# Attention's last products and the first part of its output projection on one Trainium2 core

## The chip, the cores and the metric

The kernel runs on one core of one Trainium2 chip. The metric is the device time of one execution in microseconds (us). Work is spread over TensorE (PE, with its weight loads as PEld), VectorE (DVE), ScalarE (ACT), GpSimd (POOL) and the queue of SyncE (SP), which issues every DMA of this kernel. Each engine runs its instructions in the order in which they were put on it, and waits on semaphores for the others.

## The reference

A trunk of two encoder layers over 1024 tokens of width 1024, all in float32. Only the end of the first layer's attention and the start of the cross-attention behind it matter here:

```python
o = lax.map(attend_block, qb)            # softmax(q k^T) v, 16 heads, 4 key/value heads
o = o.transpose(1, 0, 4, 2, 3, 5).reshape(b, s, N_HEADS * HEAD_DIM)
return o @ w_o                           # output projection, 1024 x 1024
...
x = x + axial_gqa_attention(rmsnorm(x, attn_norm[ia]), ...)
x = x + memory_cross_attention(rmsnorm(x, xattn_norm[i]), ...)
```

`rmsnorm` scales each row by one over its root mean square and each channel by a factor; the factors of the norm ahead of the cross-attention are `xattn_norm`.

## The kernel before

Products of two float32 matrices are made of three passes: each operand is split into a high part (ACT copies it to the reduced type, line 673 or 665) and a low part (DVE subtracts the high part from the source, line 674 or 668), and `mm3` adds high x high, high x low and low x high (lines 746 to 748). Weights come by DMA into a buffer `scr` of 128 x 1024, of which there are six (line 657), and are split from there into slots `R`.

**The attention loop** (lines 1168 to 1211) runs over 128 units: a block of 128 queries, a head. `skewed` puts the stages of several units side by side. In step s stand: the scores of unit s (PE, four matmuls into one of two banks `pA`, line 779), with the row maximum (DVE, line 789), the exponential (ACT, line 792), the reciprocal of the sum (DVE, line 794) and the scaling of the probabilities by it (POOL, line 795); the transposes of unit s-2 (PE, eight, line 740) with their split into `PT` (lines 673 and 674); and, for every second unit, the values of units s-3 and s-4 (PE, 16 matmuls into a bank `pB`, of which there are four, lines 1192 and 1193), copied out by ACT (line 1198). Two heads are then joined: a DMA on SP's queue moves 64 partitions ("crossed", line 1200), POOL adds (line 1202) and splits the pair into the left operand of the projection, `OT` (lines 1205 and 1206). So POOL has the scaling and the joining in one queue. The loop is not ordered by hand: a list scheduler of the framework takes the instructions in program order and places them by its own model, so the order on each engine around a change can differ from the text's.

**Behind the loop** `run` (lines 2118 to 2141) loads and splits the first half of the projection's weights (`load_rows`, four pieces of 512 KB, line 681), then the rows `X` of the residual (eight tiles, line 2128) with the second half's four pieces after the first two tiles, and calls `cross`, which loads the factors `xattn_norm` by a broadcast DMA (`bcast`, line 712) before its planned section.

**The projection** is interleaved with the first work of the cross-attention (`Seven.begin`, line 447). For each step (n, t) - half n of the columns, row tile t - there are `gemm` (24 matmuls into a `pB` bank), `add` (DVE adds the bank to X[t], line 1556), `save` (a store of that half of X[t] to HBM, line 314), and after n = 1 the sum of squares of the row (ACT, line 727; POOL, lines 719 and 721), the normalisation in place (DVE, line 318) and the transposes (PE, line 323). The steps start with (0, 0), (0, 2), (1, 0), (1, 2); X[0]'s transposes follow the fourth. The normalisation overwrites X[0], so it waits for both stores of X[0].

Of the kernel before, what the change touches and what calls it, by code (L numbers as in the profile page):

```python
# [10 lines left out]
F32 = mybir.dt.float32  # L11
# [5 lines left out]
P = 128  # L17
D = 1024
S = 1024
NT = S // P  # L20
# [4 lines left out]
NH = 16  # L25
# [603 lines left out]
class Kernel:  # L629
# [64 lines left out]
    def R_(self, s):  # L694
        return self.R.tiles[s] if isinstance(s, int) else s

    def load_rows(self, w, n):

        slots = [self.R.get() for _ in range(4)]
        src = w[:, n * 512:(n + 1) * 512].rearrange("(k p) n -> p k n", p=P)  # L700
        for g in range(2):
            h, l = (self.R.v(s, 4) for s in slots[2 * g:2 * g + 2])
            for k in range(2):
                self.load_w(h[:, 2 * k:2 * k + 2], l[:, 2 * k:2 * k + 2],
                            src[:, 4 * g + 2 * k:4 * g + 2 * k + 2, :], 2)
        return slots

    def bcast(self, row):

# [49 lines left out]
        return self.R.v(h, 4)[:, k % 4, cols], self.R.v(l, 4)[:, k % 4, cols]  # L759


    def attention(self):
# [6 lines left out]
        Q, prs, OT, sums = {}, {}, [], {}  # L769

        def score(u):
            j, hh, i = units[u]
# [397 lines left out]
        with tc.tile_pool(name="at", bufs=1, reuse_waits="tile") as at:  # L1170
            PT = [[at.tile([P, 2048], F32R, name=f"PT{i}{j}") for j in range(2)] for i in range(2)]
            halves = self.scr().rearrange("p (a b c) -> p a b c", a=2, b=2)
            def parts(u):
                return (x.rearrange("p (a b) -> p a b", a=8) for x in PT[u // 2 % 2])

            def turn_p(u):
                ph, pl = parts(u)
                c = slice(u % 2 * P, (u % 2 + 1) * P)
                self.transposed(prs.pop(u), lambda g, p: self.hi_lo(ph[:, 4 * g:4 * g + 4, c], pl[:, 4 * g:4 * g + 4, c], p))

            def values(u):
                j, hh, i = units[u]
                if i == 0:
                    return
                kv = hh // 4
                if hh == 0:
                    OT.append([R.get(), R.get()])
                ph, pl = parts(u)
                o = self.psB()[:, :256]
                for kt in range(NT):  # L1190
                    v = R.tiles[V[kt // 4]].rearrange("p (k h c) -> p k h c", k=4, h=4)[:, kt % 4, kv, :]
                    nc.tensor.matmul(o, v, ph[:, kt], start=kt == 0, stop=False)  # L1192
                    nc.tensor.matmul(o, v, pl[:, kt], start=False, stop=kt == NT - 1)  # L1193
# [6 lines left out]
                nc.sync.dma_start(out=far[mine], in_=own[other])  # L1200
# [12 lines left out]
        return OT  # L1213


    def memory_part(self, mT, g, t):
# [6 lines left out]
    def cross(self, i, X, steps=None, mixer=None, over={}):  # L1223

        nc, R, a = self.nc, self.R, self.a
        Xd = self.tc.dram_tile([S, D], F32, name=f"Xq{i}")
        U = Seven(self, a["xattn_w_q"][i], lambda f: (2 * f * P, (2 * f + 1) * P), X, Xd, self.bcast(a["xattn_norm"][i]))
# [9 lines left out]
        def plan_split(plan, name, f, late):  # L1239
# [877 lines left out]

    def run(self):
        nc, R, a = self.nc, self.R, self.a
        OT = self.attention()  # L2120
        ws = [self.load_rows(a["attn_w_o"][0], 0)]
        xp = self.ctx.enter_context(self.tc.tile_pool(name="xres", bufs=1, reuse_waits="tile"))
        X = [xp.tile([P, D], F32, name=f"X{t}") for t in range(NT)]
        for t in (0, 2, None, 4, 6, 1, 3, 5, 7):
            if t is None:
                ws.append(self.load_rows(a["attn_w_o"][0], 1))
            else:
                nc.sync.dma_start(out=X[t], in_=a["x"][0][t * P:(t + 1) * P, :])
# [8 lines left out]
        steps = self.rows_by(lhs, X, free, lambda n, k: self.blk(ws[n], k, slice(0, 512)), lambda n: R.put(*ws[n]))  # L2137
        lhs, *ops = self.cross(0, X, steps)
        ready = []
        gemm, add, over = self.ffn(0, lhs, X, *ops, lambda plan: ready.extend([self.pool_weights(plan)]))  # L2140
        lhs, *ops = self.cross(1, X, None, partial(self.pool_mixer, gemm, add, ready[0]), over)
        self.ffn(1, lhs, X, *ops, out=self.out[0])


# [30 lines left out]
```

## Time and profile before

| | us |
|---|---|
| three runs, median (lowest to highest) | 2510.43 (2509.54 to 2513.05) |
| the profiled execution | 2508.51 |
| its span | 2506.7 |
| PE busy | 2473.4 (99%) |
| DVE busy | 1958.6 (78%) |
| ACT busy | 1348.4 (54%) |
| attention loop, about | 160 to 528 |
| projection's first four products | 528.8 to 551.0 |

Times in the profile are us from the start of the span. A row of the timeline gives start, length, engine, line, operation, output and inputs, count, and in brackets how long the engine stood idle before it and what released it. "SPq" rows are issues of DMAs; where several are merged, the length runs from the first to the last. In a table by stage each stretch has the busy time of PE, PEld, DVE, ACT and POOL, the mean granted clock of TensorE (1.00 is full speed), the share of the 16 DMA engines and GB/s. Of a wait for several semaphores only the last to come is named.

### The profile page before, as it was taken

To read this page: it belongs to the slowest core of one execution; us is meant where nothing else is said; L and a number is where in the kernel's file an instruction comes from. 1 tells how busy PE (TensorE), PEld (TensorE's weight loads), DVE (VectorE), ACT (ScalarE), POOL (GpSimd) and SP (SyncE) were. 2 spreads that over 40 slices of the span, in tenths; PEclk is the share of its full clock that TensorE was granted. 3 is DMA by queue.
4 is the path that set the end of the run, shared out by engine and by line. 5 is a ranking of instruction groups with operands and counts; after the bars stand their busy time and mean duration, and the time that the engine had idled before them with its cause. 6 is when DMAs were issued, how large, how long until landed. Compare 5 with 4: busy or idle time off the path is not lost.

```text
span 2506.7 us, 37225 instructions
## 1 busy us (share of the span) xinstructions
PE 2473.4 (99%) x13435; PEld 2129.7 (85%) x13435; DVE 1958.6 (78%) x2899; ACT 1348.4 (54%) x2307; POOL 436.2 (17%) x594
## 2 busy tenths in 40 slices
PE   9999999999999999999999999999999999999998
PEld 8999999978898888888888888889888888887887
DVE  7779989864986379888889776987559888888875
ACT  6558888852655255555555334655335555554542
POOL 5756666631011000000000003102010000000001
PEclk9999999999999999999999999999999999999999
DMA  7100000042595124243258553388223324337852
GB/s 253 43 2 14 13 14 13 13 171 68 187 317 183 57 79 126 84 122 110 85 170 285 198 182 111 126 283 306 73 72 109 114 84 124 108 93 255 278 189 97
DMA packets 314733, 326.50 MB, mean 130 GB/s; under 512 B 14133, under 2 KB 248861, under 8 KB 314549
## 3 DMA queue, kind: packets, MB, share of 16 engines
q1 hardware_dynamic: 314549, 324.12, 39.9%
q8 instruction: 106, 1.74, 0.3%
q14 instruction: 78, 0.64, 0.1%
HBM read 232.48 MB, written 82.58 MB: 126 GB/s over the span
## 4 chain that ended last, share of the span: by engine, by line
PE 87%; issue 4%; DVE 3%; DMA 2%; ACT 2%; POOL 1%; SPq 0%; POOLq 0%; DVEq 0%; ACTq 0%
PE pB L746 21%; PE pB L748 21%; PE pB L747 21%; PE pA L779 4%; PE pB L740 4%; PE pA L748 3%; PE pA L746 3%; PE pA L747 3%; PE pB L1193 2%; PE pB L1192 2%; DVE R L668 1%; PE pB L323 1%; ACT R L665 1%; DMA scr<-in_ffn_w_down 1%; PE pA L2058 1%
## 5 line engine op out<-in xcount | busy, mean ns | idle before, releaser
L746 PE MATMUL pB<-R,R 128*128 128x512 f32 (+1 forms) x2764 | 1024.3, 371 | 8.4 <-DVE scr L439 3.3
L748 PE MATMUL pB<-R,R 128*128 128x512 f32 (+1 forms) x2760 | 1016.4, 368 | 1.3 <-DVE R L668 1.2
L747 PE MATMUL pB<-R,R 128*128 128x512 f32 (+1 forms) x2764 | 1017.3, 368 | 0.0
L746 PEld LDWEIGHTS pB<-R,R 128*128 128x128 f32 x2764 | 521.1, 189 | 100.7 <-DVE scr L439 4.6
L748 PEld LDWEIGHTS pB<-R,R 128*128 128x128 f32 x2760 | 520.1, 188 | 89.0 <-DVE R L668 2.6
L747 PEld LDWEIGHTS pB<-R,R 128*128 128x128 f32 x2764 | 521.2, 189 | 85.6 <-DVE R L674 0.4
L665 ACT ACTIVATE R<-scr 128x512 fp32r<-128x512 f32 (+2 forms) x340 | 256.9, 781 | 218.3 <-DMA scr<-Gs 60.3
L668 DVE TENSOR_TENSOR R<-scr,R 128x512 fp32r<-128x512 f32 (+2 forms) x340 | 291.6, 887 | 21.5 <-ACT R L665 20.9
L668 DVE TENSOR_TENSOR R<-X,R 128x512 fp32r<-128x512 f32 x374 | 252.5, 686 | 67.5 <-ACT R L665 66.6
L665 ACT ACTIVATE R<-X 128x512 fp32r<-128x512 f32 x374 | 231.7, 630 | 135.8 <-PE pB L747 65.4
L719 POOL TENSOR_SCALAR ms<-ss 128x1 f32<-128x1 f32 (+1 forms) x53 | 14.9, 281 | 1659.0 <-ACT R L727 1280.7
L437 ACT COPY scr<-pB 128x512 f32<-128x512 f32 x156 | 91.3, 585 | 188.3 <-PE pB L748 182.5
L673 ACT ACTIVATE PT<-pB 128x512 fp32r<-128x512 f32 x256 | 140.1, 604 | 56.0 <-PE pB L740 55.7
L789 DVE TENSOR_REDUCE nm<-pA 128x1 f32<-128x1024 f32 x125 | 152.5, 1220 | 20.5 <-PE pA L779 20.5
L674 DVE TENSOR_TENSOR PT<-pB,PT 128x512 fp32r<-128x512 f32 x256 | 163.5, 679 | 5.0 <-ACT PT L673 4.9
L1765 DVE TENSOR_TENSOR X<-pB,X 128x512 f32<-128x512 f32 (+1 forms) x145 | 99.3, 686 | 85.5 <-PE pB L748 84.5
L795 POOL TENSOR_SCALAR scr<-scr,inv 128x1024 f32<-128x1024 f32 x125 | 140.7, 1127 | 70.1 <-DVE inv L794 69.8
L746 PE MATMUL pA<-R,R 128*128 128x512 f32 (+1 forms) x420 | 150.6, 359 | 0.0
L748 PE MATMUL pA<-R,R 128*128 128x512 f32 (+1 forms) x420 | 150.2, 358 | 0.2 <-DVE R L668 0.2
L747 PE MATMUL pA<-R,R 128*128 128x512 f32 (+1 forms) x420 | 150.0, 357 | 0.0
L779 PE MATMUL pA<-R,R 128*128 128x512 f32 x512 | 145.4, 405 | 0.0
L792 ACT ACTIVATE scr<-pA,nm 128x1024 f32<-128x1024 f32 x125 | 139.8, 1118 | 1.5 <-DVE nm L789 0.5
(172 smaller groups left out, 3485.0 us busy)
## 6 DMA issues: line engine op xcount, KB each, us to landing
X<-in_ffn_w_up SPq DMA_DIRECT2D x82, 512.0 KB
Gs<-X SPq DMA_DIRECT2D x105, 256.0 KB
scr<-in_ffn_w_down SPq DMA_DIRECT2D x45, 512.0 KB
scr<-Gs SPq DMA_DIRECT2D x35, 512.0 KB
scr<-in_xattn_w_kv SPq DMA_DIRECT2D x32, 512.0 KB
scr<-Gs SPq DMA_DIRECT2D x42, 384.0 KB
Wt<-scr SPq DMA_DIRECT2D x44, 256.0 KB
Gs<-scr SPq DMA_DIRECT2D x42, 256.0 KB
```

The source lines that it names most:

```text
L665: self.nc.scalar.activation(hi, src, AF.Copy)
L668: self.nc.vector.tensor_tensor(out=lo, in0=src, in1=hi.bitcast(F32), op=OP.subtract)
L673: nc.scalar.activation(hi, src, AF.Copy)
L674: nc.vector.tensor_tensor(out=lo, in0=src, in1=hi.bitcast(F32), op=OP.subtract)
L740: self.nc.tensor.transpose(p[:, k, :], src[:, b * P:(b + 1) * P], self.ident)
L746: mm(out, ah, bh, start=start, stop=False)
L747: mm(out, ah, bl, start=False, stop=False)
L748: mm(out, al, bh, start=False, stop=stop)
L779: nc.tensor.matmul(s[:, kh * 512:(kh + 1) * 512], q, R.v(K[part][kh], 4)[:, kv], start=part == 0, stop=part == 1)
L789: nc.vector.tensor_reduce(nm, s, axis=AX.X, op=OP.max, negate=True)
L792: nc.scalar.activation(pr, s, AF.Exp, bias=nm, accum_out=rs)
L795: nc.gpsimd.tensor_scalar(pr, pr, ri, 1.0, op0=OP.mult, op1=OP.mult)
```

## The change

Two products of the projection, steps (0, 0) and (0, 2), move into the attention loop's last steps (its drain): a fifth stage of `skewed` calls what `ahead` holds for a unit, one step after its values. The first half's weight pieces hang there too, at units 112, 115, 118 and 121, with load and split together; the two products hang at units 124 and 125. `load_rows` returns four calls, one for each piece, instead of doing all at once. `steps` then skips the products already made, and their adds and saves stay where they were. The first cross-attention's factors are loaded in `run` right behind the second half's weights, among the row loads in the text; the second layer's call of `bcast` moves to the caller, to the same place in the program.

```diff
-    def load_rows(self, w, n):
-        slots = [self.R.get() for _ in range(4)]
+    def load_rows(self, w, n, slots):
         src = w[:, n * 512:(n + 1) * 512].rearrange("(k p) n -> p k n", p=P)
...
+        def part(k):
+            if not slots:
+                slots.extend(self.R.get() for _ in range(4))
+            h, l = (self.R.v(s, 4)[:, 2 * k % 4:2 * k % 4 + 2] for s in slots[k // 2 * 2:k // 2 * 2 + 2])
+            self.load_w(h, l, src[:, 2 * k:2 * k + 2, :], 2)
+        return [partial(part, k) for k in range(4)]
...
-            skewed(len(units), (0, scores), (2, turn_p), (3, values))
+            skewed(len(units), (0, scores), (2, turn_p), (3, values), (4, lambda u: ahead.get(u, lambda: None)()))
...
-        OT = self.attention()
-        ws = [self.load_rows(a["attn_w_o"][0], 0)]
+        OT, X, wo, ws, early = [], [], a["attn_w_o"][0], [[], []], ((0, 0), (0, 2))
...
+        gemm, *others = self.rows_by(lhs, X, free, lambda n, k: self.blk(ws[n], k, slice(0, 512)), lambda n: R.put(*ws[n]))
+        first, second = (self.load_rows(wo, n, ws[n]) for n in range(2))
+        last = NT * NH - 1
+        ahead = {last - 15 + 3 * k: f for k, f in enumerate(first)}
+        ahead.update({last - 3 + k: partial(gemm, *early[k]) for k in range(2)})
+        self.attention(OT, ahead)
+        xp = self.ctx.enter_context(self.tc.tile_pool(name="xres", bufs=1, reuse_waits="tile"))
+        X += [xp.tile([P, D], F32, name=f"X{t}") for t in range(NT)]
         for t in (0, 2, None, 4, 6, 1, 3, 5, 7):
             if t is None:
-                ws.append(self.load_rows(a["attn_w_o"][0], 1))
+                for f in second:
+                    f()
+                gain = self.bcast(a["xattn_norm"][0])
             else:
                 nc.sync.dma_start(out=X[t], in_=a["x"][0][t * P:(t + 1) * P, :])
+        steps = lambda n, t: (n, t) in early or gemm(n, t), *others
+        lhs, *ops = self.cross(0, X, gain, steps)
```

On PE the drain's end changes. In these rows, a piece of the difference, lines 747 and 748 are the two moved products (the rows of the first end, those of the second begin) and line 740 is the last unit's eight transposes:

```order
 L747 MATMUL pB<-R_79,R_81 128x512
 L748 MATMUL pB<-R_80,R_82 128x512
+L740 MATMUL pB<-ident,scr 128x128 x8
 L746 MATMUL pB<-R_75,R_81 128x512
 L747 MATMUL pB<-R_86,R_81 128x512
```

The last transposes now stand between the two products; before, they stood ahead of both, between the last two groups of values. The last group of values follows the second product.

On DVE, inside the loop, this is the place of the first weight piece, before:

```order
604 L789 TENSOR_REDUCE nm<-pA 128x1
605 L674 TENSOR_TENSOR PT_2589<-pB,PT_2588 128x4x128 x2
606 L789 TENSOR_REDUCE nm<-pA 128x1
607 L794 RECIPROCAL inv<-sum 128x1
608 L674 TENSOR_TENSOR PT_2587<-pB,PT_2586 128x4x128 x2
609 L794 RECIPROCAL inv<-sum 128x1
```

and now, with R_86 the low part of the piece and R_75 its high part:

```order
604 L789 TENSOR_REDUCE nm<-pA 128x1
605 L674 TENSOR_TENSOR PT_2589<-pB,PT_2588 128x4x128 x2
606 L789 TENSOR_REDUCE nm<-pA 128x1
607 L674 TENSOR_TENSOR R_86<-scr,R_75 128x1024
608 L794 RECIPROCAL inv<-sum 128x1
609 L674 TENSOR_TENSOR PT_2587<-pB,PT_2586 128x4x128
610 L794 RECIPROCAL inv<-sum 128x1
```

The piece's subtraction stands ahead of the reciprocal of the first of two units, and the second unit's comes between the two halves of a split. The other three pieces stand alike, behind a row maximum (line 789).

On SP's queue the end of the loop and the row loads before ("crossed" is the exchange of line 1200, the X are residual rows, Xq their stores):

```order
24 L1200 DMA crossed<-scr 64x256
25 L681 DMA scr<-in_attn_w_o 128x2x512 x2
26 L1200 DMA crossed<-scr 64x256
27 L681 DMA scr<-in_attn_w_o 128x2x512 x2
28 L2128 DMA X_7404<-in_x 128x1024
29 L2128 DMA X_7406<-in_x 128x1024
30 L681 DMA scr<-in_attn_w_o 128x2x512 x2
31 L2128 DMA X_7408<-in_x 128x1024
```

and now:

```order
30 L1200 DMA crossed<-scr 64x256
31 L681 DMA scr<-in_attn_w_o 128x2x512 x3
32 L1200 DMA crossed<-scr 64x256
33 L681 DMA scr<-in_attn_w_o 128x2x512
34 L712 DMA scr<-in_xattn_norm 128x1024
35 L1200 DMA crossed<-scr 64x256
36 L2142 DMA X_7454<-in_x 128x1024
37 L2142 DMA X_7456<-in_x 128x1024
38 L2142 DMA X_7458<-in_x 128x1024
```

The second half's weights and the factors now stand ahead of the last exchange, and the row loads directly behind it, as the first X loads did before. Behind X's stores the queue is as it was, and so is the order on PE behind the transposes of X[0].

More of the change, by code (lines that the diff above doesn't have):

```diff
@@ L759, in blk, with attention @@
         return self.R.v(h, 4)[:, k % 4, cols], self.R.v(l, 4)[:, k % 4, cols]
-    def attention(self):
+    def attention(self, OT, ahead):
         nc, R, a, tc = self.nc, self.R, self.a, self.tc
@@ L768, in attention @@
         units = [(j, hh, i) for j in range(NT // 2) for hh in range(NH) for i in range(2)]
-        Q, prs, OT, sums = {}, {}, [], {}
+        Q, prs, sums = {}, {}, {}
         def score(u):
@@ L1221, in quarter, with cross @@
         return (self.R.hv(h).rearrange("p (k n) -> p k n", k=4)[:, k % 4, cols] for h in hs[k // 4 * 2:k // 4 * 2 + 2])
-    def cross(self, i, X, steps=None, mixer=None, over={}):
+    def cross(self, i, X, gain, steps=None, mixer=None, over={}):
         nc, R, a = self.nc, self.R, self.a
         Xd = self.tc.dram_tile([S, D], F32, name=f"Xq{i}")
-        U = Seven(self, a["xattn_w_q"][i], lambda f: (2 * f * P, (2 * f + 1) * P), X, Xd, self.bcast(a["xattn_norm"][i]))
+        U = Seven(self, a["xattn_w_q"][i], lambda f: (2 * f * P, (2 * f + 1) * P), X, Xd, gain)
         plan_sums = self.down_sums(i)
@@ L2119, in run @@
         nc, R, a = self.nc, self.R, self.a
-        OT = self.attention()
-        ws = [self.load_rows(a["attn_w_o"][0], 0)]
[L2122 to L2125, printed above, removed]
-                ws.append(self.load_rows(a["attn_w_o"][0], 1))
-            else:
-                nc.sync.dma_start(out=X[t], in_=a["x"][0][t * P:(t + 1) * P, :])
+        OT, X, wo, ws, early = [], [], a["attn_w_o"][0], [[], []], ((0, 0), (0, 2))
         def lhs(t, k):
@@ L2135, in free @@
                 R.put(*OT[t // 4 * 2 + t % 2])
-        steps = self.rows_by(lhs, X, free, lambda n, k: self.blk(ws[n], k, slice(0, 512)), lambda n: R.put(*ws[n]))
-        lhs, *ops = self.cross(0, X, steps)
+        gemm, *others = self.rows_by(lhs, X, free, lambda n, k: self.blk(ws[n], k, slice(0, 512)), lambda n: R.put(*ws[n]))
[6 more added lines that the diff above has]
+        X += [xp.tile([P, D], F32, name=f"X{t}") for t in range(NT)]
+        for t in (0, 2, None, 4, 6, 1, 3, 5, 7):
+            if t is None:
+                for f in second:
+                    f()
+                gain = self.bcast(a["xattn_norm"][0])
+            else:
+                nc.sync.dma_start(out=X[t], in_=a["x"][0][t * P:(t + 1) * P, :])
+        steps = lambda n, t: (n, t) in early or gemm(n, t), *others
+        lhs, *ops = self.cross(0, X, gain, steps)
         ready = []
         gemm, add, over = self.ffn(0, lhs, X, *ops, lambda plan: ready.extend([self.pool_weights(plan)]))
-        lhs, *ops = self.cross(1, X, None, partial(self.pool_mixer, gemm, add, ready[0]), over)
+        lhs, *ops = self.cross(1, X, self.bcast(a["xattn_norm"][1]), None, partial(self.pool_mixer, gemm, add, ready[0]), over)
         self.ffn(1, lhs, X, *ops, out=self.out[0])
```

7 lines of the change are left out of this document (removed).

## Prediction

> **What bounds the kernel now.** I read the page first, then the table by stage, then the timeline and the DMA queue's own issues from 480 to 560 us, where the first layer's attention hands over to its output projection.
>
> ```profile
> PE 2473.4 (99%) x13435; PEld 2129.7 (85%) x13435; DVE 1958.6 (78%) x2899; ACT 1348.4 (54%) x2307; POOL 436.2 (17%) x594
> 400.00:450.00 50.00, 50.00 (x368) 45.92 (x368) 45.43 (x75) 42.31 (x83) 32.09 (x37) 1.00 0.05 13
> 522.40:528.80 6.40, 4.78 (x26) 4.34 (x26) 4.14 (x5) 3.35 (x5) 1.65 (x2) 0.75 0.60 212
> 528.80:551.00 22.20, 22.20 (x97) 17.87 (x96) 9.58 (x9) 7.79 (x9) 3.49 (x5) 0.99 0.90 344
> 551.00:554.70 3.70, 0.16 (x2) 0.01 (x1) 1.35 (x2) 0.00 (x0) 0.00 (x0) 1.00 0.05 20
> ```
>
> In the table's rows stand the stretch, its length, the busy time of PE, PEld, DVE, ACT and POOL, the granted clock, the DMA share and GB/s. PE is busy for 99% of the span, so only its few holes can be won. In the attention loop (400 to 450) it has none, and DVE is busy for 45.4 us of 50. The change touches two holes behind the loop: the drain (522.4 to 528.8) and the wait at 551. Call V125 and V127 the last two groups of 16 products of probabilities and values, T127 the eight transposes between them, X0 the first tile of residual rows.
>
> ```profile
> 520.28 0.38 PE L1192 MATMUL pB<-PT,R 128*128 128x256 f32 x1
> 522.13 0.28 PE L1193 MATMUL pB<-PT,R 128*128 128x256 f32 x1
> 523.38 1.09 PE L740 MATMUL pB<-ident,scr 128*128 128x128 f32 x8 [0.97 <-POOL scr L795]
> 524.78 0.38 PE L1192 MATMUL pB<-PT,R 128*128 128x256 f32 x1 [0.31 <-ACT PT L673]
> 525.51 0.50 PE L1193 MATMUL pB<-PT,R 128*128 128x256 f32 x1 [0.34 <-DVE PT L674]
> 528.79 0.51 PE L746 MATMUL pB<-R,R 128*128 128x512 f32 x1
> 533.39 0.19 PEld L747 LDWEIGHTS pB<-R,R 128*128 128x128 f32 x1 [0.39 <-DVE R L674]
> ```
>
> V125 ends at 522.41 (its last row), the projection starts at 528.79. V127 and T127 need about 1.9 us (V125's first row to its last, plus one step) and 0.9 us; the drain takes 6.4. Part of the rest is waiting, part a halved clock:
>
> ```profile
> 524.00:526.00 2.00, 1.35 (x8) 0.91 (x7) 1.24 (x2) 1.87 (x3) 0.44 (x1) 0.90 0.39 106
> 526.00:528.00 2.00, 2.00 (x12) 2.00 (x11) 1.86 (x3) 1.11 (x2) 0.29 (x1) 0.50 0.92 341
> 528.00:530.00 2.00, 2.00 (x10) 1.82 (x10) 0.55 (x1) 0.97 (x2) 0.00 (x0) 0.74 0.30 112
> 554.00:556.00 2.00, 1.31 (x10) 1.27 (x11) 1.23 (x2) 0.68 (x1) 0.00 (x0) 1.00 0.00 0
> ```
>
> The clock costs 0.1, 0.5 and 0.26 of 2 us: 1.7 us. After the wait at 551 it is 1.00.
>
> **The drain: won.** Two products of the projection now stand on PE between V125, T127 and V127. Their left sides are two of the first query blocks, long done; their weights must be split before V125 ends, and the last split stands on DVE ahead of V125's. While PE multiplies, POOL scales the last unit's probabilities, and ACT and DVE split first the second half's four weight pieces and then these. So the three waits go and PE stays busy, at full clock: 6.4 - 2.8 = 3.6 us, and 0.3 of the wait at 533.39, whose weights are early now: **-3.9 us**. V127 could be late behind those pieces: it starts 5.55 + 0.9 + 5.55 = 12 us after V125's end (a product is a quarter of the 22.2 us row); the last piece's load is issued some 2 us after that end, behind V125's exchange, and landing, two splits and the last unit's own need about 4 + 2.3 + 1.3 us, estimated from the rows below. Some 2 us are left, so I take nothing; without that cover it costs what is missing.
>
> **The wait for X0: longer.** The hole at 551 is the transposes of X0 waiting for its normalisation (L318), which writes X0 in place and so waits until both halves of the unnormalised rows are stored.
>
> ```profile
> 529.43 0.47 SPq L1200 DMA_DIRECT2D crossed<-scr  x1
> 530.01 1.05 SPq L681 DMA_DIRECT2D scr<-in_attn_w_o  x2
> 531.12 0.93 SPq L2128 DMA_DIRECT2D X<-in_x  x2
> 532.15 1.27 SPq L681 DMA_DIRECT2D scr<-in_attn_w_o  x2
> 533.51 5.56 SPq L2128 DMA_DIRECT2D X<-in_x  x6
> 546.47 0.32 SPq L314 DMA_DIRECT2D Xq<-X  x1
> 553.35 1.28 DVE L318 SCALAR_TENSOR_TENSOR X<-X,rs,scr 128x1024 f32<-128x1024 f32 x1 [6.91 <-DMA Xq<-X]
> 554.69 1.09 PE L323 MATMUL pB<-ident,X 128*128 128x128 f32 x8 [3.54 <-DVE X L318]
> 535.00:550.00 15.00, 15.00 (x68) 12.42 (x67) 6.89 (x7) 4.66 (x6) 0.75 (x2) 1.00 1.02 405
> scr<-in_attn_w_o SPq DMA_DIRECT2D x8, 512.0 KB
> X<-in_x SPq DMA_DIRECT2D x8, 512.0 KB
> Xq<-X SPq DMA_DIRECT2D x14, 256.0 KB
> scr<-in_xattn_norm SPq DMA_DIRECT2D x1, 512.0 KB
> ```
>
> The store issued at 546.47 is waited for until 553.35, 6.9 us, because it stands behind loads that fill the DMA engines (share 1.02, 405 GB/s). Measure from the last exchange of halves ("crossed", 529.43): behind it lie four weight loads, eight row loads and the factors, 13 x 0.524 MB, and three stores of 0.262 MB: 7.6 MB, 18.8 us at 405 GB/s, of the 23.9 us to L318. The other 5.1 us are issue, the first landing and the tail.
>
> After the change only the eight rows and three stores lie behind that exchange: 4.98 MB, 12.3 us, so L318 starts 17.4 us after it, or 16.3 if the tail shrinks with the broadcast load moved ahead. I take 16.8. The rows themselves can't go earlier: they stand behind the exchange on SP's queue, the exchange waits for V127, and V127 now comes behind two products. That is where the change gives back what it wins. The products that used to cover the loads (22.2 us for four, 5.55 each) are halved: two of them, 11.1 us, starting some 0.45 us before the exchange's issue (V127's copy lies between), so PE is free 10.65 us after it. X0's transposes come 1.34 us after L318 starts (553.35 to 554.69), at 18.1. PE stands 7.5 us where it stood 3.7: **+3.8 us**, between +3.3 and +4.4.
>
> **The loop: slower.** Four pieces of weights are split inside the last 16 units, every third unit. The loop's pace, and the price of the same split outside it:
>
> ```profile
> 501.96 1.23 DVE L789 TENSOR_REDUCE nm<-pA 128x1 f32<-128x1024 f32 x1 [0.34 <-PE pA L779]
> 507.44 1.23 DVE L789 TENSOR_REDUCE nm<-pA 128x1 f32<-128x1024 f32 x1 [0.34 <-PE pA L779]
> 530.39 1.23 DVE L674 TENSOR_TENSOR R<-scr,R 128x1024 fp32r<-128x1024 f32 x1 [1.84 <-ACT R L673]
> 530.77 1.06 ACT L673 ACTIVATE R<-scr 128x1024 fp32r<-128x1024 f32 x1 [0.41 <-DMA scr<-in_attn_w_o]
> ```
>
> Two units take 5.48 us (501.96 to 507.44). DVE gets 4 x 1.23 = 4.9 us more. In 44 us (16 units) it has 9% free, 4.0 us, so by capacity alone 0.9 us is too much. But the free time comes in gaps like these 0.34 us, in which DVE waits, and the order puts the piece ahead of the reciprocal. Reciprocal, POOL's scaling and PE's transposes are a chain with little slack. The trace shows what a delay there does:
>
> ```profile
> 505.43 0.15 DVE L794 RECIPROCAL inv<-sum 128x1 f32<-128x1 f32 x1
> 505.75 1.13 POOL L795 TENSOR_SCALAR scr<-scr,inv 128x1024 f32<-128x1024 f32 x1 [1.33 <-DVE inv L794]
> 507.25 1.03 PE L740 MATMUL pB<-ident,scr 128*128 128x128 f32 x8
> 487.91 0.15 DVE L794 RECIPROCAL inv<-sum 128x1 f32<-128x1 f32 x1
> 489.57 2.22 POOL L795 TENSOR_SCALAR scr<-scr,inv 128x1024 f32<-128x1024 f32 x2
> 490.74 1.09 PE L740 MATMUL pB<-ident,scr 128*128 128x128 f32 x8 [0.85 <-POOL scr L795]
> ```
>
> Normally POOL starts 0.32 us after the reciprocal and ends 0.37 us before the transposes. At 487.9 an exchange was late, POOL started 1.66 us after it, 1.34 late, and PE stood 0.85 us: slack of some 0.5, the rest lost. A piece holds the reciprocal by 1.2 us (DVE alone) to 2.3 us (DVE waiting for ACT's half first), so a piece costs 0.7 to 1.8 us, four cost 2.8 to 7.3. The exponential behind ACT's half is late as well, but PE's next scores have two banks. I take 1.0 each, nearest to the measured 0.85: **+4.0 us**, with 0.9 and 7.3 as ends. The loads cost nothing here: on a queue at a share of 0.05 (the row from 400) each is issued, by the order, more than a unit pair ahead of its split.
>
> **The clock: one more half-speed stretch.** A gap of 3.5 us left the clock at 1.00, the broken-up drain halved it. A gap of 7.5 us is twice the one that did no harm; I take the drain's price, **+1.7 us**, between 0 and 3.4. [...]
>
> **Factors and the rest.** The first factors' load is counted above as bytes moved ahead; the second layer's load keeps its place. Behind X0's transposes PE's order is unchanged to the end, and it waits little there, mostly for engines fed by PE:
>
> ```profile
> PE pB L746 <- DVE scr L439: 3.3, 6, 1.0
> ```
>
> So a shift of X0's transposes goes through whole.
>
> **Sum.** -3.9 + 3.8 + 4.0 + 1.7 = +5.6 us on the profiled execution's 2508.51 us (span 2506.7, 1.8 around it): 2514.1. It lies 1.9 us under the median of the runs shown, 2510.43, so the forecast in runs is 2516.0 us, 0.22% slower.
>
> **Rivals.**
> - *The loop takes the pieces in* (chance 0.20). If DVE's 4.0 us of free time are usable, the loop pays 0.9: +2.5, 2512.9 us. For it: DVE and ACT each have free time. Against it: the 0.85 us at 490.74, where both had it as well.
> - *The stores don't wait for the rows* (0.09; the other side). If X0's last store were served at once, L318 would start 3 us or less after the add, inside the second product's 5.55 us, and PE wouldn't stand: -3.9 - 3.7 + 4.0 = -3.6, 2506.8 us, and with a loop at 0.9 -6.7, 2503.7 us. It decides where that store lands within some 3 us of its issue. Against it: the 6.9 us at 553.35, in a queue filled in the same order.
> - *No half clock* (0.10): +3.9, 2514.3 us. For it: the row at 554.
> - *The pieces run in series with the loop* (0.09): 7.3 instead of 4.0, +8.9, 2519.3 us. The order's pieces ahead of reciprocals speak for it, the 0.5 us of slack against.
> - *The products don't fill the drain* (0.02): if the first needed a weight split late, PE would stand anyway; the order excludes it.
>
> **How the numbers follow.** 0.2% is 5.0 us, about what a measurement of this kernel can tell from no change: faster is under 2505.4, slower over 2515.4. The forecast has 0.50; with its terms' ends (3.3 to 4.4, 2.8 to 5.5, 0.8 to 2.5) it runs from 2513 to 2519.5, some two thirds of it over the bound: 0.35; with the serial case and the half clock's worse end slower is 0.46. Faster is the part of the second rival in which the loop absorbs as well, 0.05. The rest, 0.49, lies within. The range from 2509.0 to 2520.0 leaves out the second rival and the far ends.
>
> **What would show it.** Right: no wait between V125 and V127 in the changed kernel and clock 1.00 there; row loads issued right behind the last exchange; PE standing 7 to 8 us ahead of X0's transposes on the store, and a half clock after it; V125 ending some 4 us later, with PE waiting for POOL's scaling four times. Wrong: a wait at X0 of under 4 us, or a loop with its old 5.48 us for two units.

## The result, and the profile after

The changed kernel takes 2517.34 us in the median of 7 runs (2516.61 to 2521.29), the kernel before 2510.43 us (2506.59 to 2513.05, 7 runs): a ratio of 1.003, 95% interval 1.0019 to 1.0042. It is slower by 6.9 us. The profiled executions have spans of 2515.8 and 2506.7 us.

The first part of the changed kernel's page (busy time of each engine, share of the span, instructions): PE is busy 3.3 us longer, in a span that is 9.1 us longer.

```profile
PE 2476.7 (98%) x13435; PEld 2131.0 (85%) x13435; DVE 1958.3 (78%) x2899; ACT 1347.1 (54%) x2307; POOL 432.8 (17%) x594
```

The table by stage (length, busy time of PE, PEld, DVE, ACT and POOL, clock, DMA share, GB/s), cut where the phases end: the loop at its old pace, V125's end to V127's end, the products behind it, and the hole ahead of X0's transposes:

```profile
400.00:450.00 50.00, 50.00 (x368) 45.93 (x367) 45.43 (x73) 42.29 (x83) 32.24 (x37) 1.00 0.05 13
527.00:540.68 13.68, 13.68 (x75) 11.72 (x73) 6.13 (x7) 5.48 (x7) 2.03 (x4) 1.00 0.44 155
540.68:551.74 11.06, 11.06 (x50) 8.82 (x48) 1.98 (x3) 1.52 (x3) 2.62 (x5) 1.00 0.80 302
551.74:560.44 8.70, 0.00 (x1) 0.00 (x0) 1.34 (x2) 0.00 (x0) 0.00 (x0) 0.71 0.57 198
```

The drain is full: PE is busy for all of 13.68 us, at clock 1.00. The hole ahead of X0 is now 8.70 us, and the clock falls in it. The queue's issues and the timeline around that hole:

```profile
541.27 0.47 SPq L1200 DMA_DIRECT2D crossed<-scr  x1
541.83 4.01 SPq L2142 DMA_DIRECT2D X<-in_x  x8
546.01 0.69 DVE L1555 TENSOR_TENSOR X<-pB,X 128x512 f32<-128x512 f32 x1 [9.09 <-DMA X<-in_x]
559.10 1.28 DVE L318 SCALAR_TENSOR_TENSOR X<-X,rs,scr 128x1024 f32<-128x1024 f32 x1 [10.54 <-DMA Xq<-X]
560.44 1.97 PE L323 MATMUL pB<-ident,X 128*128 128x128 f32 x8 [8.70 <-DVE X L318]
```

The eight rows are issued right behind the last exchange (541.27), X0's normalisation waits for its store until 559.10, 17.8 us after that issue, and the eight transposes take 1.97 us where they took 1.09: they run at half clock. It lasts until about 565.6:

```profile
560.00:562.00 2.00, 1.56 (x8) 1.56 (x9) 0.99 (x2) 0.93 (x1) 0.00 (x0) 0.50 0.07 28
562.00:564.00 2.00, 2.00 (x7) 1.62 (x7) 0.82 (x1) 2.00 (x6) 0.75 (x2) 0.50 0.27 103
564.00:566.00 2.00, 2.00 (x7) 1.57 (x6) 1.66 (x3) 0.16 (x1) 0.00 (x0) 0.59 0.00 0
```

The loop. A unit pair's values start at 475.88 us in the kernel before and at 476.38 in the changed one; V125's start at 520.28 and 525.04. So 0.5 us were there before any piece, and the pieces cost 48.66 - 44.40 = 4.26 us. The table by stage between these points, the kernel before first:

```profile
475.88:520.28 44.40, 43.39 (x319) 39.41 (x317) 39.47 (x65) 36.62 (x73) 27.82 (x33) 1.00 0.06 14
476.38:525.04 48.66, 45.44 (x320) 39.19 (x318) 44.55 (x69) 41.05 (x79) 28.47 (x32) 1.00 0.18 56
```

DVE gets 5.1 us more where it had 4.9 free, and is now busy for 44.55 of 48.66 us: it still stands for 4.1 of them. PE stands 3.2 us where it stood 1.0: 2.2 of the 4.26 us. The other 2.05 stand in the longer busy time of as many products; what that time was stays open. Rows of the changed kernel, with the first piece in them:

```profile
476.38 0.36 PE L1192 MATMUL pB<-PT,R 128*128 128x256 f32 x1
494.12 0.21 ACT L792 ACTIVATION_READ_ACCUMULATOR scr<-pA,nm 128x1 f32 x1
494.21 1.07 ACT L673 ACTIVATE R<-scr 128x1024 fp32r<-128x1024 f32 x1
495.31 1.23 DVE L674 TENSOR_TENSOR R<-scr,R 128x1024 fp32r<-128x1024 f32 x1
496.45 0.16 DVE L794 RECIPROCAL inv<-sum 128x1 f32<-128x1 f32 x1
496.81 2.22 POOL L795 TENSOR_SCALAR scr<-scr,inv 128x1024 f32<-128x1024 f32 x2 [3.68 <-DVE inv L794]
525.04 0.39 PE L1192 MATMUL pB<-PT,R 128*128 128x256 f32 x1 [0.59 <-DVE PT L674]
```

The sum of an exponential is ready at 494.3, its reciprocal comes at 496.45, behind the piece, and POOL has stood 3.68 us for it (2.31 us at the same scaling before). Two units' scalings then run back to back.

### The profile page after: what moved, and what is told of

The parts are those of the page before. It is cut to its first block, busy times and chain, and to the rows that moved or that the text cites. A ratio compares the mean times of both kernels' runs of the same rounds, so it can differ in the third digit from the quotient of the medians.

```text
span 2515.8 us, 37201 instructions
## 1 busy us (share of the span) xinstructions
PE 2476.7 (98%) x13435; PEld 2131.0 (85%) x13435; DVE 1958.3 (78%) x2899; ACT 1347.1 (54%) x2307; POOL 432.8 (17%) x594
## 4 chain that ended last, share of the span: by engine, by line
PE 85%; DVE 5%; issue 4%; ACT 3%; DMA 2%; POOL 1%; POOLq 0%; SPq 0%; DVEq 0%; ACTq 0%
PE pB L746 21%; PE pB L748 20%; PE pB L747 20%; PE pA L779 4%; PE pB L740 4%; PE pA L748 3%; PE pA L746 3%; PE pA L747 3%; PE pB L1193 2%; PE pB L1192 2%; DVE R L668 2%; ACT R L665 1%; PE pB L323 1%; DMA X<-in_ffn_w_up 1%; PE pA L2057 1%
```

## The experiments

Twelve kernels, held against the kernel before, whose median was 2510.2 to 2511.3 us in the three comparisons. "Loop's loss" below is, as above, V125's first product less the first product of a unit pair ahead of any piece, less the 44.40 us of the kernel before.

| kernel | median us | ratio to before, 95% | loop's loss | PE stands at X0 |
|---|---|---|---|---|
| changed | 2517.3 | 1.0030 (1.0019 to 1.0042) | 4.26 | 8.70 |
| rows_late | 2506.7 | 0.9989 (0.9980 to 0.9997) | 3.9 | 0.65 |
| rows_four | 2510.4 | 0.9998 (0.9990 to 1.0007) | 4.6 | 2.88 |
| gain_late | 2517.5 | 1.0023 (1.0014 to 1.0032) | 4.6 | 8.46 |
| before_rows | 2505.5 | 0.9978 (0.9969 to 0.9987) | 0 | 0 |
| pieces_only | 2507.6 | 0.9988 (0.9979 to 0.9997) | 4.4 | 0 |
| halves | 2516.7 | 1.0028 (1.0018 to 1.0038) | 4.0 | 8.70 |
| no_low | 2514.8 | 1.0016 (1.0008 to 1.0025) | 1.4 | 8.26 |
| no_low_rows | 2505.2 | 0.9981 (0.9971 to 0.9990) | 2.0 | 0.79 |
| halves_rows_pool | 2504.6 | 0.9973 (0.9962 to 0.9983) | 0.55 | 1.66 |
| half_products | 2506.0 | 0.9981 (0.9972 to 0.9990) | 2.2 | 0 |
| warm_mm | 2516.1 | 1.0022 (1.0012 to 1.0032) | 4.1 | PE kept busy |
| warm_tr | 2516.0 | 1.0021 (1.0012 to 1.0030) | 3.9 | PE kept busy |

### Does X0's store wait for the rows?

**rows_late.** Theory: the store stands behind the row loads. Six of them move behind X2's store:

```diff
-        for t in (0, 2, None, 4, 6, 1, 3, 5, 7):
+        for t in (0, 2, None):
...
+        def freed_rows(n, t):
+            freed(n, t)
+            if (n, t) == (0, 4):
+                for r in (4, 6, 1, 3, 5, 7):
+                    nc.sync.dma_start(out=X[r], in_=a["x"][0][r * P:(r + 1) * P, :])
```

> The changed kernel with six of the eight row loads (all but X0 and X2) issued only behind X2's store, after the product (0,4). Theory (X0's store is late because it stands behind row loads): with one other load ahead of it the store lands some 2 to 4 us after its issue at about 547, L318 starts by 551, PE stands 0 to 1.5 us in place of 8.7 us and no half clock follows (it cost 2.4 us): 2517.3 - 7.7 - 2.4 = about 2507 us. Rival 1 (the store takes its 10 us whatever is queued): the wait stays over 7 us, 2516 to 2518 us. Rival 2 (the deferred rows come late for the additions of X4 and X6): the wait at X0 goes, and PE stands some 4 us one or two products later: about 2511 us.

Measured: 2506.7 us, 10.6 less than the changed kernel. Its timeline:

```profile
540.03 0.47 SPq L1200 DMA_DIRECT2D crossed<-scr  x1
540.59 1.04 SPq L2142 DMA_DIRECT2D X<-in_x  x2
549.80 1.29 DVE L318 SCALAR_TENSOR_TENSOR X<-X,rs,scr 128x1024 f32<-128x1024 f32 x1 [2.48 <-DMA Xq<-X]
551.15 1.09 PE L323 MATMUL pB<-ident,X 128*128 128x128 f32 x8 [0.65 <-DVE X L318]
552.13 3.18 SPq L2149 DMA_DIRECT2D X<-in_x  x6
```

L318 starts 9.8 us behind the exchange's issue instead of 17.8, the transposes take 1.09 us again, and PE doesn't stand for the later rows. Both rivals fall: the store doesn't take its 10 us by itself, and the deferred rows aren't late.

**rows_four** has four rows ahead, four behind (the two tuples become `(0, 2, None, 4, 6)` and `(1, 3, 5, 7)`).

> The changed kernel with four row loads (X0, X2, X4, X6) ahead and the other four behind X2's store: a dose between the changed kernel (eight ahead, L318 17.8 us behind the last exchange's issue, PE standing 8.7 us) and rows_late (two ahead, 9.8 us, 0.65 us). Theory (each 0.52 MB load ahead of the store costs 1.34 us): L318 starts 12.4 us behind the exchange's issue, X0's transposes 13.8 us behind it, PE stands some 3.2 us, and the half clock may or may not follow: 2506.7 + 2.6 = about 2509.3 us, to 2511 with the half clock. Rival (what counts is that loads are on the queue at all, or the rows deferred to just the right place): a wait near 0.7 or near 8.7 us.

Measured: 2510.4 us. The exchange is issued at 540.67:

```profile
552.67 1.29 DVE L318 SCALAR_TENSOR_TENSOR X<-X,rs,scr 128x1024 f32<-128x1024 f32 x1 [4.85 <-DMA Xq<-X]
554.02 1.09 PE L323 MATMUL pB<-ident,X 128*128 128x128 f32 x8 [2.88 <-DVE X L318]
```

L318 comes 12.0 us behind the issue (12.4 expected). Two, four and eight loads ahead of the store give 9.8, 12.0 and 17.8 us: 1.1 to 1.5 us for each load, 1.34 on average. It is a dose, not a threshold. In the profile of rows_four X0's transposes take 1.09 us after the 2.9 us wait, as at clock 1.00 in the kernel before, and the span is only 1.8 us over that of rows_late. The medians are 3.7 us apart; 0.7 of it is the kernel before's own difference between the two comparisons. The profiled execution was the fastest of its eleven (2507.51 us), and the mean granted clock on record for each execution is 0.999 in 6 of 11 of rows_late and in 2 of 11 of rows_four, lower in the rest. So the others ran longer at a lowered clock; at which place isn't shown.

**gain_late** puts the first factors' `bcast` behind the row loads in the text, as before the change.

> The changed kernel with the first factors' load at its old place behind the eight rows: 0.52 MB more lie between the last exchange and X0's store. Theory: L318 starts 1.3 us later and PE stands 10.0 us in place of 8.7: 2517.3 + 1.3 = about 2518.6 us. Rival (the load's place doesn't matter): 2517.3 us with a wait of 8.7 us.

Measured: 2517.5 us, a wait of 8.46 us. But the experiment doesn't tell: on the queue the factors still stand ahead of the last exchange, as in the changed kernel (530.13 and 541.27).

```profile
531.46 0.43 SPq L712 DMA_DIRECT2D scr<-in_xattn_norm  x1
542.32 0.47 SPq L1200 DMA_DIRECT2D crossed<-scr  x1
```

The framework's scheduler put the load there with the line in either place. So the run is a repeat of the changed kernel, and what the factors' place is worth wasn't measured.

**before_rows** is rows_late's edit in the kernel before.

> The kernel before with the same six row loads issued behind X2's store. Theory (the store is late because of the loads): the 3.5 us wait at X0 goes: about 2507.3 us. Rival (the wait at X0 is the chain of load, addition, store and normalisation itself, which the four weight loads delay as well): 1 to 3 us stay, 2508 to 2510 us.

Measured: 2505.5 us. PE doesn't stand at X0 (no idle time on its row), so the wait of 3.5 us had the same cause, with two more products to cover it:

```profile
548.95 1.28 DVE L318 SCALAR_TENSOR_TENSOR X<-X,rs,scr 128x1024 f32<-128x1024 f32 x1 [2.80 <-DMA Xq<-X]
550.70 1.03 PE L323 MATMUL pB<-ident,X 128*128 128x128 f32 x8
```

It is 5.1 us under the kernel before, more than the wait of 3.5 us. In this profile the drain's clock is 1.00 and the projection starts 7.08 us behind V125's first product (520.97 to 528.05), against 8.51 at half clock in the kernel before; how often other executions have that stretch isn't shown. It is also 1.2 us under rows_late (intervals overlap): with the rows late, nothing is left of the change's gain as it was written.

### What do the pieces cost in the loop, and why?

**pieces_only** keeps the pieces and moves no product.

```diff
-        OT, X, wo, ws, early = [], [], a["attn_w_o"][0], [[], []], ((0, 0), (0, 2))
+        OT, X, wo, ws, early = [], [], a["attn_w_o"][0], [[], []], ()
```

> The changed kernel with its four weight pieces split in the loop and no product moved into the drain. Theory (the pieces delay the chain in the loop, whatever the drain does): V127's values start some 4 us later than before; the drain keeps its 6.4 us and its half clock; four products again lie behind the exchange and cover rows and store, so that the wait at X0 (3.5 us before) goes: 2510.8 + 4.3 - 0.3 - 3.5 = about 2511 us. Rival (the loop's loss comes from the drain's products meeting the pieces): the loop keeps its pace of 5.48 us for two units, about 2507 us.

Measured: 2507.6 us, the rival's figure, but not for its reason: the loop loses 4.4 us as the theory has it. The sum missed the drain:

```profile
526.15 0.38 PE L1192 MATMUL pB<-PT,R 128*128 128x256 f32 x1 [0.59 <-DVE PT L674]
530.64 0.39 PE L1192 MATMUL pB<-PT,R 128*128 128x256 f32 x1 [1.49 <-ACT PT L673]
534.37 0.47 SPq L1200 DMA_DIRECT2D crossed<-scr  x1
552.61 1.28 DVE L318 SCALAR_TENSOR_TENSOR X<-X,rs,scr 128x1024 f32<-128x1024 f32 x1 [2.70 <-DMA Xq<-X]
554.46 1.03 PE L323 MATMUL pB<-ident,X 128*128 128x128 f32 x8
```

Its table by stage, in the gap between V125 and V127:

```profile
528.00:530.00 2.00, 1.15 (x11) 0.91 (x9) 0.28 (x2) 1.23 (x3) 1.41 (x3) 1.00 1.02 369
```

With four products (22.2 us) ahead of X0's transposes, these start at 554.46: V125 starts 6.1 us before those products, 8.5 in the kernel before. That is 2.4 us less. Some 1.4 of it go with the clock, which stays at 1.00 as in before_rows (7.08). The rest is an order that I didn't expect: five of the first product's 24 matmuls stand on PE behind V127's first row (530.86 to 532.01) and fill a part of its wait. The eight rows are again issued right behind the last exchange (534.37), but with four products behind it X0's second half is added so late (549.22) that L318 then waits 2.70 us for its store, not 10.54, and PE doesn't stand. So of the two moves, it was the products that lengthened the wait.

**halves** cuts the loop's four pieces into eight, one in every second unit.

```diff
+        def small(k):
+            if k % 4 == 0:
+                slots.extend(self.R.get() for _ in range(2))
+            h, l = (self.R.v(s, 4)[:, k % 4:k % 4 + 1] for s in slots[k // 4 * 2:k // 4 * 2 + 2])
+            rv = self.scr()[:, :512].rearrange("p (a b) -> p a b", a=1)
+            self.nc.sync.dma_start(out=rv, in_=src[:, k:k + 1, :])
+            self.hi_lo(h, l, rv)
```

> The changed kernel with the first four weight pieces cut into eight of half the size, one in every second unit of the loop. Theory (a piece costs what its delay of the reciprocal exceeds the chain's slack of some 0.5 us): half a piece delays it 0.6 to 1.2 us and costs 0.1 to 0.6, eight cost about 1.6 in place of 4.25: 2517.3 - 2.6 = about 2514.7 us. Rival (the loop pays DVE's and ACT's time for the pieces, however they are cut): the loop loses 4 us or more as before, 2517 to 2519 us.

Measured: 2516.7 us, a loop's loss of 4.0 us, half a microsecond for every half piece. My theory, that the slack swallows small delays, falls for these pieces. The groups of DVE between 478 and 524 us (count, busy us, mean ns):

```profile
L674 DVE TENSOR_TENSOR PT<-pB,PT 128x512 fp32r<-128x512 f32 x30 | 19.7, 679 | 0.6 <-ACT PT L673 0.6
L674 DVE TENSOR_TENSOR R<-scr,R 128x512 fp32r<-128x512 f32 x8 | 7.4, 922 | 0.7 <-ACT R L673 0.7
```

The same subtraction of the same size takes 679 ns on average from PSUM and 922 ns from `scr`. Its rows beside POOL's show where the longer ones stand:

```profile
479.60 1.12 POOL L803 TENSOR_SCALAR scr<-scr,inv 128x1024 f32<-128x1024 f32 x1 [0.30 <-DVE inv L802]
479.80 1.47 DVE L674 TENSOR_TENSOR R<-scr,R 128x512 fp32r<-128x512 f32 x1 [0.36 <-ACT R L673]
491.53 0.69 DVE L674 TENSOR_TENSOR R<-scr,R 128x512 fp32r<-128x512 f32 x1 [0.31 <-ACT R L673]
491.59 1.62 POOL L803 TENSOR_SCALAR scr<-scr,inv 128x1024 f32<-128x1024 f32 x1
```

At 479.80 DVE's piece starts inside POOL's scaling and ends 0.55 us behind its end (480.72), 0.8 us late; at 491.59 POOL's scaling starts inside DVE's piece and takes 1.62 us instead of 1.12. In both pairs the one that starts second takes longer; by what mechanism isn't shown. The other six subtractions go alike: three that meet no GpSimd instruction take 0.68 us, and three that start inside one end 0.53 to 0.55 us behind its end, as the row at 479.80 does. The delays of the four add up to 1.9 us on DVE; how much of it reaches PE isn't shown. The 30 splits of `PT`, from `pB`, don't show it: they take 679 ns on average, about what a subtraction from `scr` takes that meets no GpSimd instruction (0.68 us).

**no_low** leaves DVE's half of the four pieces out: the subtraction isn't done, and the first half's products read the high part twice.

```diff
-            self.load_w(h, l, src[:, 2 * k:2 * k + 2, :], 2)
+            if n:
+                self.load_w(h, l, src[:, 2 * k:2 * k + 2, :], 2)
+            else:
+                rv = self.scr().rearrange("p (a b) -> p a b", a=2)
...
+                nc.scalar.activation(h, rv, AF.Copy)
```

> The changed kernel without the DVE half of the four pieces split in the loop: ACT still writes their high parts, the subtraction is left out, and the first half's products read the high part in place of the low one (part of the computation is changed). The other four pieces are split as before. Theory (DVE's 1.23 us per piece is what the loop loses): V125 starts at most 1 us later than before, where the pieces moved it by 4.2 us, and the rest stays: 2517.0 - 3.5 = about 2513.5 us. Rival (ACT's 1.06 us ahead of the exponential is what the loop loses): the loop still loses 2 to 4 us, 2515 to 2517 us.

Measured: 2514.8 us, a loop's loss of 1.4 us, between the two. **no_low_rows** adds rows_late's edit.

> The same without the DVE half of the loop's pieces, and with six row loads behind X2's store as in rows_late. What is left of the change then is the filled drain, to be held against before_rows (2505.5 us), which has the late rows and the old drain. Theory (the drain was worth some 3.9 us in waits and clock): 2506.7 - 3.5 = about 2503 us, 2 to 3 us under before_rows. Rival (the drain's products win nothing that the old drain did not already have, or the loop's loss is ACT's): 2505 to 2507 us.

Measured: 2505.2 us, a loop's loss of 2.0 us. So the two theories share it: some 2.8 of 4.26 us (no_low against the changed kernel) or 1.9 of 3.9 (no_low_rows against rows_late) go with DVE's subtraction, and the rest with what is left, ACT's copies ahead of the exponential. The second run also prices the drain: from V125's first product to the third product of the projection are 15.67 us (521.91 to 537.58), less 11.1 for the two products 4.6, against 7.08 in before_rows (520.97 to 528.05). The drain wins 2.5 us there, and the loop and X0 give back 2.0 and 0.8: nothing is left, and the medians (2505.2 and 2505.5 us, intervals overlapping) tell no difference.

**halves_rows_pool** is halves with the late rows, and with the subtraction on GpSimd.

```diff
-            self.hi_lo(h, l, rv)
+            self.nc.scalar.activation(h, rv, AF.Copy)
+            self.nc.gpsimd.tensor_tensor(out=l, in0=rv, in1=h.bitcast(F32), op=OP.subtract)
```

> rows_late with the loop's pieces cut into eight halves, whose subtraction GpSimd does in place of DVE. By two of its rows of a quarter of a piece (0.74 us each) half a piece takes it some 1.5 us. Theory (POOL has the time: it is idle for 18 of 50 us in the loop, and DVE's part of the loss, some 2.3 us of 4.2, goes): 2506.7 - 2 = about 2504.7 us. Rival (POOL's scaling stands behind the subtraction, and the chain has no room for it): each half loses 0.5 to 1.0 us, the loop 4 to 8 us, 2507 to 2511 us.

Measured: 2504.6 us, the lowest median of all, 6.7 us under the kernel before in the same comparison. The loop loses 0.55 us: V125 starts 44.95 us behind the pair ahead of the pieces. The table by stage over that stretch, first of halves, then of this run:

```profile
476.67:525.08 48.41, 44.58 (x320) 39.08 (x318) 45.98 (x73) 41.65 (x81) 28.73 (x33) 1.00 0.18 52
475.75:520.70 44.95, 43.93 (x319) 39.33 (x317) 39.64 (x65) 40.68 (x81) 37.31 (x40) 1.00 0.19 55
```

POOL's groups between 478 and 524 us show the pieces at 1.29 us, dearer than on DVE, and scalings that wait for little but the reciprocals:

```profile
L804 POOL TENSOR_SCALAR scr<-scr,inv 128x1024 f32<-128x1024 f32 x17 | 19.0, 1125 | 5.6 <-DVE inv L803 5.5
L714 POOL TENSOR_TENSOR R<-scr,R 128x512 fp32r<-128x512 f32 x8 | 10.3, 1292 | 0.0
```

So the loss hangs on the engine that does the subtraction, not on what one subtraction takes. On POOL it holds no reciprocal; but it also leaves DVE, which is busy for 45.98 of 48.41 us in halves and had 4.9 us free before, for an engine with more room. How much of DVE's part was the place in its queue, how much its lack of free time and how much the longer instructions where DVE and GpSimd overlap (1.9 us on DVE in halves) was not taken apart. ACT copies all eight halves here too, and no more than 0.55 us is lost: what no_low lost with whole pieces doesn't follow from ACT's work alone. Against before_rows (0.9978, 0.9969 to 0.9987) the interval overlaps (0.9973, 0.9962 to 0.9983): with most of its costs mended (0.55 us in the loop and 1.66 at X0 are left), the filled drain is worth about 1 us by the medians, and that is not told apart from nothing.

**half_products**, on rows_late: only the first four of eight blocks of each moved product, so that two pieces suffice.

```diff
-        ahead = {last - 15 + 3 * k: f for k, f in enumerate(first)}
-        ahead.update({last - 3 + k: partial(gemm, *early[k]) for k in range(2)})
+        ahead = dict(zip((last - 9, last - 6, last - 1, last), first))
+        ahead.update({last - 3 + k: partial(gemm, *early[k], range(4)) for k in range(2)})
```

> rows_late with only the first halves (four of eight blocks) of the products (0,0) and (0,2) moved into the drain, so that two pieces instead of four are split in the loop; the other two pieces are loaded and split in the drain. Theory (a piece costs the loop 1.05 us, and 5.5 us of products are enough for the drain's 3.6 us): 2506.7 - 2.1 = about 2504.6 us. Rival (the pieces pushed into the drain make V127 or the rest of the two products wait): what the loop wins is lost there, 2506 to 2508 us.

Measured: 2506.0 us. Two pieces cost the loop 2.2 us (2.1 expected), and PE doesn't stand at X0, but V127 waits for its split behind the pushed-in pieces:

```profile
533.41 0.39 PE L1192 MATMUL pB<-PT,R 128*128 128x256 f32 x1 [1.07 <-DVE PT L674]
```

Part of the win goes there, the rival's way; against rows_late the interval overlaps, so it is not told apart.

### Does the standing PE halve the clock?

**warm_mm** and **warm_tr** fill the hole ahead of X0's transposes with work whose result nobody reads, 36 products or 72 transposes.

```diff
+        def freed_warm(n, t):
+            if (n, t) == (1, 2):
+                extra = self.psB()
+                for k in range(12):
+                    self.mm3(extra, *lhs(t, k % 8), *self.blk(ws[n], k % 8, slice(0, 512)), True, True)
+            freed(n, t)
```

(warm_tr: `for k in range(72): nc.tensor.transpose(extra[:, k % 4 * P:(k % 4 + 1) * P], self.ident, self.ident)`.)

> The changed kernel with 36 further products of 512 columns (their result is read by nobody) behind the product (1,2), about 8.3 us of the 8.7 us in which PE stands for X0. Theory (the half clock after the wait comes from the standing PE): X0's transposes start when they did, within 0.5 us, at clock 1.00, and 2.4 us come back: about 2514.7 us. Rival (the half clock has another cause, as the one in the second layer): 2517 us.

> The changed kernel with 72 transposes of the identity in the same place, about 8.4 us of PE time by 0.117 us each. If any work of PE holds the clock, the half clock goes as with the products: about 2514.7 us. If transposes do not hold it, the rows after the wait stay at 0.50 and the time at about 2517 us, and where the transposes themselves run at half clock they end after X0 is ready and cost up to some 4 us more: 2517 to 2521 us. [...]

Measured: 2516.1 and 2516.0 us. The half clock is gone in both: the granted clock is 1.00 in every 2 us from 552 to 566 us, where the changed kernel has 0.50 from 556 to 564. X0's transposes in the timeline of warm_mm:

```profile
560.63 1.09 PE L323 MATMUL pB<-ident,X 128*128 128x128 f32 x8 [0.83 <-DVE X L318]
```

And of warm_tr, where nothing but transposes runs on PE for 8 us, first the timeline, then the table by stage:

```profile
551.45 8.02 PE L2149 MATMUL pB<-ident 128*128 128x128 f32 x72
560.24 1.09 PE L323 MATMUL pB<-ident,X 128*128 128x128 f32 x8 [0.77 <-DVE X L318]
```

```profile
554.00:556.00 2.00, 2.00 (x21) 2.00 (x19) 0.00 (x0) 0.00 (x0) 0.00 (x0) 1.00 1.00 381
560.00:562.00 2.00, 1.76 (x12) 1.62 (x13) 0.79 (x2) 1.13 (x3) 0.00 (x0) 1.00 0.17 69
```

X0's transposes start when they did (560.44) and take 1.09 us. So the standing PE caused the half clock here, and 72 transposes of f32 hold it at 1.00 as 36 products do, the first of the two cases expected; that is shown for a clock that was at 1.00 ahead of them. The price in the medians is 1.2 to 1.4 us (the intervals of the ratios overlap); the spans fall by 1.7 and 2.0 us (2514.1 and 2513.8). That is less than the 2.4 us I expected; 1.0 of those were won back later in the changed kernel's profile too (below).

## Why the prediction was right, point by point

The forecast was 2516.0 us, the median is 2517.3. Between the two profiles, by the start of the same work in each:

| step | forecast | measured | from |
|---|---|---|---|
| ahead of the pieces | 0 | +0.5 | 475.88, 476.38 |
| loop | +4.0 | +4.3 | V125's start less that |
| drain | -3.9 | -4.4 | 8.51 (520.28 to 528.79) to 4.54 (525.04 to 540.68, less 11.1), and the 0.39 at 533.39 |
| wait for X0 | +3.8 | +5.2 | 3.54 to 8.70 |
| half clock behind it | +1.7 | +2.4 | X0's transposes are 5.75 us later (554.69, 560.44), X2's 8.2 |
| the rest of the program | 0 | +0.9 | 9.1 at the end |

The sum came to 5.6 us, the medians differ by 6.9, the two profiles by 9.1 (the measured rows give 8.9; the other 0.2 lie between them).

- **Drain: right, with a caution.** No wait between V125 and V127, clock 1.00. But 1.7 us of the win were a half clock that only the profile of the kernel before shows: before_rows has the same gaps, pieces_only has similar ones, and both have clock 1.00. Held against before_rows, the filled drain wins 2.5 us (no_low_rows). The cover that I named for V127 (2 us left) held.
- **Wait for X0: right mechanism, too small.** I took 16.8 us from the exchange's issue to L318, out of 16.3 to 17.4; it was 17.8. The bytes were right (1.34 us for each row load, against 1.29 by 405 GB/s). What failed is "if the tail shrinks with the broadcast load moved ahead": the part that is not bytes was 17.8 - 12.3 = 5.5 us, not under 5.1. The products that cover it ran out 10.5 us behind the issue (551.74), by my count 10.65.
- **Loop: right size, wrong picture of the slack.** 1.07 us for a piece, 1.0 forecast; that was the price of one other delay in the trace, so that it fits so well is in part luck. The reciprocal was held 2.1 us, within my 1.2 to 2.3. The sign that I named, PE waiting for POOL's scaling four times, didn't show: between 476.38 and 525.04 it waits for POOL 1.00, 0.35 and 0.85 us (0.85 and 0.16 before), for DVE 0.17 and 0.59 and for ACT 0.22. And the "slack of some 0.5", from which I had the lower end, gave halves nothing. That a third to a half of the loss stays without DVE's subtraction, and that it or POOL's scaling takes longer where the two overlap (in halves 1.47 us in place of 0.68, 1.62 in place of 1.12), I didn't have.
- **Clock: right, too small in place.** The 1.7 us was borrowed from the drain's stretch; that it comes near is luck, not a working. Half speed lay over X0's transposes and up to 565.6, 2.4 us; by 1551 us 1.0 of it had been won back (X's transposes there are 7.2 us later), by what was not traced.
- **Not foreseen:** a second half-speed stretch, in the second layer, worth 1.5 us of the profile's 9.1 (below). It isn't the change's alone: before_rows has it without the change.
- **The factors' load:** I counted the bytes as moved ahead by the change's line; in gain_late the scheduler moves them without that line.
- **The rivals.** "The loop takes the pieces in" fails by 4.3 against 0.9 us; "in series" (7.3) fails as well; "no half clock" fails by the rows at 0.50, and "the products don't fill the drain" by its 13.68 us. "The stores don't wait for the rows" is the one that was worth trying to make true: rows_late does so, and the 2506.7 us measured there are close to that rival's 2506.8.

## What to carry to other kernels

Work moved into a hole may have been the cover of a later wait: count what still lies ahead of that wait, and what is queued ahead of the transfer it waits for; here the order of six loads was worth more than the whole change (10.6 against 6.9 us). A tight loop's spare time on an engine is of little use if it is no larger than the added work (here 4.9 us free on DVE and 5.1 added, of which the loop lost 4.3) and the added instruction stands in the queue ahead of the one that the bottleneck waits for. So look for an engine whose queue has room at that place (here GpSimd, 0.55 us in place of 4.0), not for the one with the cheapest instruction (0.92 us on DVE, 1.29 on GpSimd). And a stretch of half clock in one profile is to be looked for in a second profile with the same gaps (here 0.50 in the kernel before, 1.00 in before_rows) before it is booked as a cost that can be won.

## What the runs showed of the hardware

- In the changed kernel the clock fell to half within 8.70 us of standing PE: it is 1.00 from 552 to 554 us, 0.85 from 554 to 556 and 0.50 from 556 to 564, and X0's transposes take 1.97 us. They take 1.97 us in no_low too, behind 8.26 us of standing. Behind the 2.88 us of rows_four and the 3.54 us of the kernel before they take 1.09 us; the clock is 1.00 behind the latter.
- It also fell without any standing. In the changed kernel PE is busy for all of the 10 us from 1578 to 1588 (timeline, then table by stage), and yet the clock is 0.50 from 1584 to 1586:

```profile
1577.38 1.04 PE L323 MATMUL pB<-ident,X 128*128 128x128 f32 x8
1578.25 3.82 PE L2057 MATMUL pA<-scr 128*128 128x112 f32 x32
```

```profile
1582.00:1584.00 2.00, 2.00 (x13) 2.00 (x13) 0.00 (x0) 0.80 (x2) 0.01 (x1) 0.70 0.00 0
1584.00:1586.00 2.00, 2.00 (x11) 2.00 (x11) 0.69 (x1) 0.00 (x0) 0.00 (x0) 0.50 0.00 0
1586.00:1588.00 2.00, 2.00 (x18) 2.00 (x17) 1.32 (x2) 0.54 (x1) 0.00 (x0) 0.94 0.00 0
```

It starts 0.6 us behind 32 products with 112 columns (3.82 us) in the changed kernel, and 1.3 us behind them in before_rows; over the 15 us around it the clock is 0.89 in both. The kernel before, rows_late and halves_rows_pool have 1.00 there. Why some and not others stays open. It costs 1.5 us where it falls: 17 products take 3.53 us (1582.71 to 1586.24, and in before_rows 1571.18 to 1574.71), and 17 of them take 2.0 us behind it.
- The scatter between executions goes with the clock. By the mean clock of each of 90 executions of the kernel before, the mean time is 2513.8 us at 0.996 (9 of them), 2511.7 at 0.997, 2510.3 at 0.998 and 2508.4 at 0.999 (20). So how much the clock is lowered differs between executions of one kernel, and a profile shows one of them.
- In halves five of the eight DVE subtractions from `scr` overlap a GpSimd instruction, and the one that starts second takes 0.3 to 0.8 us longer: four times the subtraction (0.97 to 1.47 us in place of 0.68), once POOL's scaling (1.62 in place of 1.12).
